# Two low-rank projections side by side, and k and r of two column blocks projected from the unnormalised input

## The chip, the cores and the metric

The kernel runs on one core of one Trainium2 chip. The metric is the device time of one execution in microseconds (us). A core has a matrix engine (TensorE, PE in the profile; its weight loads are listed apart as PEld), three engines for elementwise work (VectorE = DVE, ScalarE = ACT, GpSimd = POOL), and SyncE (SP), which here only starts transfers (DMA). Each engine runs its own instructions in the order in which they were compiled and waits on semaphores for the others.

## The reference, cut to what matters

One block of a streaming encoder on x of 512 tokens by 1024 channels, all in float32:

```python
h  = rms_norm(x, norm1_g)                # y = x * rsqrt(mean(x*x) + 1e-6) * g
p  = h @ w_in                            # all projections of three branches
# branch a: gated short convolution (3 taps);  branch b: RG-LRU (4 tap convolution, gates, scan)
# branch c: RWKV-7 with 16 heads of 64, and its columns are token-shifted first
def token_shift(p, mu):
    prev = jnp.pad(p, ((0, 0), (1, 0), (0, 0)))[:, :-1]
    return p + (prev - p) * mu
r, k, v, xw, xa, xg = _split(pc, (1024, 1024, 1024, 64, 64, 128))
w_log = -softplus(-(w0 + tanh(xw) @ w2)) - 0.5   # decay = exp(-exp(w_log))
a = sigmoid(a0 + xa @ a2)
g = sigmoid(xg) @ g2
kk = k * k_k / norm_per_head(k * k_k);  k = k * (1 + (a - 1) * k_a)
# recurrence over tokens, state of 64x64 per head; then head norm, gates, merge of the branches,
# w_out, residual, second RMSNorm, MLP with squared ReLU (1024 -> 4096 -> 1024), final RMSNorm
```

The columns xw and xa together are one block of 128 columns, the low-rank block lr0; xg is the other, lr1. RMSNorm multiplies every token by one number, so a projection may be taken on x times the gain alone and multiplied by that number afterwards.

## The kernel before, in words

**Layout.** Activations are transposed, 128 channels on the partitions and 512 tokens along the free axis. Eight such tiles (kt = 0 to 7) make up the input xT. Float32 products are made from two parts per operand, hi and lo: `mm3` (lines 169 to 171) issues hi by hi, hi weight by lo input, lo weight by hi input. One projection of 128 columns is 8 kt by 3 = 24 matmuls of 128x512. Its weight is one transfer of 128x1024 (512 KB) started by SP (`load_w`), then split: ACT casts `whi` (L148), DVE subtracts to get `wlo` (L105). There are two buffers for `raw`, three each for `whi` and `wlo`.

**Helpers.** `tt` and `stt` record every tensor-tensor and scalar-tensor-tensor operation of DVE, so all of these have line 105 or 108, and a reader goes by tile names. `proj_raw` projects the input times its gain (`xgh`, `xgl`); `unscaled` multiplies the result by `rsb`, the per-token factor of the norm, and `shift` applies the token shift (one ACT operation, one DVE operation). `proj` is the ordinary projection, of the normalised `hh` and `hl`, which `pro_scale` makes: two DVE operations and one ACT operation per kt.

**The prologue (lines 207 to 383).** Two warm-up matmuls (`wu`) run on a zero tile. Per kt, ACT makes `xgh` and the square `sq`, DVE makes `xgl`; the squares of two kt are added (DVE) and summed over channels by a float32 matmul with ones into `pst`: four such matmuls. The squares and their matmuls stand under a raised priority. The three matmuls of lr0 follow per kt. The second low-rank weight is loaded after all of xT, and its projection (lr1) runs after that of lr0. Then `rsqrt_rows` turns `pst` into `rsb`. k0 and r0 (block 0 of k and r) are projected by `proj_raw`; lr0's result is evacuated (tile us0, shifted into `lr`), and `lws` and `las`, the hi and lo inputs of the second low-rank stage, are made from it (four operations over ACT and DVE). Then `pro_scale`, the evacuation of lr1 (us1), of k0 and of r0 follow.

**krv, and what is woven into it.** `krv(g)` prepares k, r, v of the 4 heads of group g, in column blocks j = 2g and 2g+1. Per block it projects k and r (not for j = 0), computes decay and a from `lws` and `las` with four matmuls (`pw`, `pa`), the head norm of k (`pn`), and products of these; then it projects v for two blocks, sums `pb`, transposes v (`pV`), and writes its results to buffers in memory. `amat(g)` makes the per-chunk matrices of the group (tile `AXt`, evacuated in two halves of four operations each), `inverse` inverts triangles, `chain` runs the recurrence. `ab(q)` is the work of branches a and b, 8 column blocks in 232 steps; it serves as filler.

**What sets the order.** The program is written as generators; `weave(crit, fill, r)` lets r filler steps follow each step of the critical generator, which gets a raised priority. The compiler's scheduler orders each engine's instructions by priority. R0 = 0.85 is the ratio for `weave(krv(0), ab)`.

**Other pieces at the start.** POOL clears a zero tile `zer`, and four transfers (L874) fill a quarter of the buffer `ttd` with zeros from it; the scheduler has put them at the very start. Near the end of the source, `ac.activation(epst, epst, AF.Sqrt)` and a memset (L1056, L1057) stand before the last stage; the scheduler has put the activation, with its table load, at the start as well. PSUM has three buffers for projections (tag pp), two for small results (pm), and one each of pu, pS and py.

## Time and profile before

| | |
|---|---|
| time, median of 3 runs | 1028.8 us (1027.36 to 1030.81) |
| profiled execution | 1029.49 us, of which the span of the profile is 1027.7 us |
| PE | 1007.2 us busy (98%), 6110 instructions |
| PEld | 817.7 us (80%) |
| DVE | 735.1 us (72%), 1251 instructions |
| ACT | 512.9 us (50%), 757 instructions |
| POOL | 110.1 us (11%), 179 instructions |
| DMA | 151.53 MB, mean 147 GB/s |

A row such as "7.57 1.75 PE L274 MATMUL pst<-sq,ones ... x2 [2.62 <-DVE sq L105]" of the timeline gives the start, the length, the engine, the line, the operation with output and inputs, the shapes, the count of instructions put together, and in brackets the idle time just before and what ended it. Rows of the windows give start and end of a stretch, its length, and for PE, PEld, DVE, ACT and POOL the busy time with the number of instructions, then the granted TensorE clock (1.00 is full speed), the mean busy share of the 16 DMA engines and GB/s. In the list of waits a row gives engine, tile and line, what ended the wait, the idle time, how often, and the longest single one. Consecutive matmuls overlap in the records: a length of 0.39 us goes with a start every 0.23 us.

### The profile page before, as it was taken

The page shows a single profiled execution, that of the slowest core. Times are in us where ns is not written, and L with a number is a line of the kernel's source. Part 1 is how long each engine was busy: PE and PEld are TensorE (multiplying, and loading weights), DVE is VectorE, ACT ScalarE, POOL GpSimd, SP SyncE. Part 2 cuts the span into 40 slices and gives each one's busy share as a digit, 9 for nine tenths or more (in the row PEclk, how much of TensorE's full clock was granted, in tenths as well). Part 3 has the DMA queues.
Part 4 walks back from the last instruction along what each step waited for, and adds up shares of the span by engine and source line. Part 5 has one row for each costly group of instructions (what it writes and reads, how often), then busy time and mean ns, then how long its engine had stood idle before and what let it go on. Part 6 is the DMA issues. An engine that isn't in the chain of part 4 may idle for free. (4 is left out here: it accounts for less than half of the span.)

```text
span 1027.7 us, 15699 instructions
## 1 busy us (share of the span) xinstructions
PE 1007.2 (98%) x6110; PEld 817.7 (80%) x6110; DVE 735.1 (72%) x1251; ACT 512.9 (50%) x757; POOL 110.1 (11%) x179
## 2 busy tenths in 40 slices
PE   8999999999999999999999999999999999999997
PEld 5777877888887788888787877888888888878885
DVE  6997497599865886794668779656554546887775
ACT  7756453655554655456446344435433334454344
POOL 1013011201212112001322100100000000000001
PEclk9999999999999999999999999999999999999999
DMA  6444643734546446434897724544333325644442
GB/s 231 129 123 112 185 134 114 215 107 128 150 134 164 136 126 161 158 95 122 268 256 243 220 87 119 174 132 130 90 99 103 98 87 164 226 127 139 143 166 102
DMA packets 49177, 151.53 MB, mean 147 GB/s; under 512 B 6544, under 2 KB 10128, under 8 KB 48080
## 3 DMA queue, kind: packets, MB, share of 16 engines
q1 hardware_dynamic: 34816, 99.93, 30.6%
q0 software_dynamic: 13568, 49.56, 18.0%
q8 instruction: 48, 0.79, 0.3%
q10 hardware_dynamic: 720, 1.05, 0.3%
q14 instruction: 25, 0.20, 0.1%
HBM read 123.78 MB, written 26.74 MB: 146 GB/s over the span
## 5 line engine op out<-in xcount | busy, mean ns | idle before, releaser
L148 ACT CAST whi<-raw 128x1024 fp32r<-128x1024 f32 (+1 forms) x164 | 169.7, 1037 | 257.0 <-PE pp L170 86.7
L105 DVE TENSOR_TENSOR wlo<-raw,whi 128x1024 fp32r<-128x1024 f32 (+1 forms) x176 | 206.5, 1175 | 91.2 <-ACT whi L148 90.6
L169 PE MATMUL pp<-hh,whi 128*128 128x512 f32 x688 | 271.2, 395 | 0.4 <-DVE rs L108 0.4
L170 PE MATMUL pp<-hl,whi 128*128 128x512 f32 x688 | 270.1, 393 | 0.0
L171 PE MATMUL pp<-hh,wlo 128*128 128x512 f32 x688 | 269.1, 391 | 0.2 <-DVE wlo L105 0.2
L169 PEld LDWEIGHTS pp<-hh,whi 128*128 128x128 f32 x688 | 129.1, 188 | 28.9 <-DVE rs L108 0.9
L171 PEld LDWEIGHTS pp<-hh,wlo 128*128 128x128 f32 x688 | 129.2, 188 | 27.5 <-DVE wlo L105 0.6
L170 PEld LDWEIGHTS pp<-hl,whi 128*128 128x128 f32 x688 | 129.2, 188 | 26.3
L169 PE MATMUL p<-h2h,whi 128*128 128x512 f32 x256 | 100.4, 392 | 0.0
L171 PE MATMUL p<-h2h,wlo 128*128 128x512 f32 x256 | 99.7, 389 | 0.0
L170 PE MATMUL p<-h2l,whi 128*128 128x512 f32 x256 | 99.6, 389 | 0.0
L108 DVE SCALAR_TENSOR_TENSOR r<-p,rsb 128x512 f32<-128x512 f32 x32 | 22.0, 691 | 69.3 <-PE p L171 68.8
L171 PEld LDWEIGHTS p<-h2h,wlo 128*128 128x128 f32 x256 | 48.1, 188 | 10.2
L169 PEld LDWEIGHTS p<-h2h,whi 128*128 128x128 f32 x256 | 48.1, 188 | 9.8
L170 PEld LDWEIGHTS p<-h2l,whi 128*128 128x128 f32 x256 | 48.1, 188 | 9.6
L1225 POOL TENSOR_TENSOR x0f<-xr,fgt 128x512 f32<-128x512 f32 x4 | 5.2, 1296 | 310.6 <-DMA raw<-in_w 301.4
L170 PE MATMUL acc<-ml,whi 128*128 128x512 f32 x64 | 25.0, 391 | 0.0
L171 PE MATMUL acc<-mh,wlo 128*128 128x512 f32 x64 | 25.0, 390 | 0.0
L1076 PE MATMUL acc<-whi,a2h 128*128 128x512 f32 x64 | 24.9, 389 | 0.0
L1076 PE MATMUL acc<-whi,a2l 128*128 128x512 f32 x64 | 24.9, 389 | 0.0
L1076 PE MATMUL acc<-wlo,a2h 128*128 128x512 f32 x64 | 24.9, 389 | 0.0
L1076 PE MATMUL acc<-whi,ah 128*128 128x512 f32 x64 | 24.9, 389 | 0.0
(368 smaller groups left out, 1733.5 us busy)
## 6 DMA issues: line engine op xcount, KB each, us to landing
raw<-in_win SPq DMA_DIRECT2D x88, 512.0 KB, 3.6
raw<-in_w SPq DMA_DIRECT2D x64, 512.0 KB, 3.6
ax<-axd POOLq DMA_DIRECT2D x8, 1024.0 KB, 10.0
axd<-AXt POOLq DMA_DIRECT2D x12, 512.0 KB, 8.7
raw<-in_w SPq DMA_DIRECT2D x24, 256.0 KB, 2.9
bkd<-BKT POOLq DMA_DIRECT2D x4, 1024.0 KB, 15.4
raw<-in_wout SPq DMA_DIRECT2D x8, 512.0 KB, 3.6
bk<-bkd POOLq DMA_DIRECT2D x7, 512.0 KB, 13.0
```

Of the source, the lines that this page charges most:

```text
L105: return v.tensor_tensor(out=o, in0=a, in1=b, op=op)
L108: return v.scalar_tensor_tensor(out=o, in0=a, scalar=s, in1=b, op0=op0, op1=op1)
L148: ac.copy(hi[:, sl], raw[:, sl])
L169: pe.matmul(ps, wh, xh, start=start, stop=False)
L170: pe.matmul(ps, wh, xl, start=False, stop=False)
L171: pe.matmul(ps, wl, xh, start=False, stop=stop)
L1076: pe.matmul(b[i], x_[:, ms], w_, start=id(b[i]) not in begun, stop=last and n == 2, skip_group_check=True)
L1225: gp.tensor_tensor(out=o0, in0=x0, in1=fgt[0], op=MUL)
```

## The change: what it does

1. The ratio R0 goes from 0.85 to 1.8. The warm-up matmuls go from 2 of 512 columns to 12 of 128.
2. Both low-rank weights are loaded first (one half through ACT's queue) and projected side by side inside the loop over kt; the squares come after them in each kt, without a raised priority, and are added in fours: two `pst` matmuls in place of four, six additions in place of four.
3. k and r of block 1 are projected in the prologue by `proj_raw`, evacuated by `unscaled` and `shift` into two tiles, and `krv(0)` uses them in place of projections of its own. The `vs` tiles, which share those tiles' buffers, are made later.
4. The zero fill of `ttd` is taken from a new tile `zz` and stands after `krv(0)`.
5. The activation with Sqrt on `epst` and its memset are gone.

```diff
--- before.py
+++ after.py
@@ -27,8 +27,8 @@
 N_KRV = 22
 FILL = {1: (4, 13, 5), 2: (36, 13, 5), 3: (4, 13, 5)}
 
-R0, R1, R2, R3 = 0.85, 0.8, 0.85, 1.6
-NWARM = 2
+R0, R1, R2, R3 = 1.8, 0.8, 0.85, 1.6
+NWARM = 12
 
 NL = 2
 NPAIR, NPS = 12, 8
@@ -240,39 +240,56 @@
     gp.memset(ones, 1.0)
     n1t = pro.tile([P, KT], F32, name="n1t")
     ac.dma_start(n1t, par[:, PI["n1"]])
-    wlr = [new_w()]
-    load_half(wlr[0], win[CN[("lr", 0)]], 0)
-    for a, n in ((0, 1), (1, 1), (2, 2)):
+    wlr = [new_w(), new_w()]
+    lr_src = [win[CN[("lr", i)]] for i in range(2)]
+
+    def load_lr(eng, i, h):
+        sl = slice(h * S, (h + 1) * S)
+        eng.dma_start(wlr[i][0][:, sl], lr_src[i][:, sl])
+
+    def load_x(a, n):
         sy.dma_start(xT[:, a:a + n], xt[a:a + n].rearrange("k p t -> p k t"))
-    load_half(wlr[0], win[CN[("lr", 0)]], 1)
-    for a, n in ((4, 2), (6, 2)):
-        sy.dma_start(xT[:, a:a + n], xt[a:a + n].rearrange("k p t -> p k t"))
-    wlr.append(new_w())
-    for i in range(2):
-        load_half(wlr[1], win[CN[("lr", 1)]], i)
+
+    load_lr(sy, 0, 0)
+    load_lr(ac, 1, 0)
+    load_x(0, 1)
+    load_x(1, 1)
+    load_x(2, 2)
+    load_lr(sy, 0, 1)
+    load_lr(sy, 1, 1)
+    load_x(4, 2)
+    load_x(6, 2)
     gp.memset(epst[:, 0:1], EPS)
     one = cp.tile([P, 1], F32, name="one")
     gp.memset(one, 1.0)
     wu = pc.tile([P, S], F32, tag="pu", name="wu")
     for i in range(NWARM):
-        pe.matmul(wu, ones, zer, start=True, stop=True)
+        pe.matmul(wu[:, 0:P], ones, zer[:, 0:P], start=True, stop=True)
     pst = pm.tile([P, S], F32, tag="pm", name="pst")
     warm = pro.tile([P, 1], F32, name="warm")
     ac.activation(warm, epst[:, 0:1], AF.Tanh)
 
-    t_lr0 = pp.tile([P, S], F32, tag="pp", name="pp")
+    t_lr = [pp.tile([P, S], F32, tag="pp", name="pp") for _ in range(2)]
+    t_lr0, t_lr1 = t_lr
     sqp_ctx = ExitStack()
     sqp = sqp_ctx.enter_context(tc.tile_pool(name="sqp", bufs=1))
     for kt in range(KT):
-        sq = (p1 if kt % 2 else sqp).tile([P, S], F32, tag=f"v{kt // 2 % 2}" if kt % 2 else f"sq{kt // 2}", name="sq")
+        if kt % 4 == 0:
+            for w in wlr:
+                split_w(w, slice(kt // 4 * S, kt // 4 * S + S))
         ac.activation(xgh(kt), xT[:, kt], AF.Copy, scale=n1t[:, kt:kt + 1])
         stt(xgl[:, kt], xT[:, kt], n1t[:, kt:kt + 1], f(xgh(kt)), MUL, SUB)
-        with tc.high_priority(offset=OFFP):
-            ac.activation(sq, xT[:, kt], AF.Square)
-            if kt % 2 == 1:
-                tt(sq, sq, sq_, ADD)
-                pe.matmul(pst, ones, sq, start=kt == 1, stop=kt == KT - 1)
-        mm3(t_lr0, *wslice(wlr[0], kt), xgh(kt), xgl[:, kt], start=kt == 0, stop=kt == KT - 1)
+        for w, t in zip(wlr, t_lr):
+            mm3(t, *wslice(w, kt), xgh(kt), xgl[:, kt], start=kt == 0, stop=kt == KT - 1)
+        sq = (p1 if kt % 2 else sqp).tile([P, S], F32, tag=f"v{kt // 2 % 2}" if kt % 2 else f"sq{kt // 2}", name="sq")
+        ac.activation(sq, xT[:, kt], AF.Square)
+        if kt % 2 == 1:
+            tt(sq, sq, sq_, ADD)
+        if kt % 4 == 3:
+            tt(sq, sq, sq4, ADD)
+            pe.matmul(pst, ones, sq, start=kt == 3, stop=kt == KT - 1)
+        if kt % 4 == 1:
+            sq4 = sq
         sq_ = sq
     with tc.high_priority(offset=OFFP):
         rsqrt_rows(pro, rsb, pst, EPS, 1.0 / D)
@@ -341,8 +358,6 @@
         tt(o, t, rsb, MUL)
         return o
 
-    t_lr1 = pp.tile([P, S], F32, tag="pp", name="pp")
-    proj_raw(wlr[1], t_lr1)
     omul = p1.tile([P, 2], F32, name="omul")
 
 
@@ -362,6 +377,12 @@
     proj_raw(load_w(win[CN[("k", 0)]]), t_k0)
     t_r0 = pc.tile([P, S], F32, tag="pS", name="r0")
     proj_raw(load_w(win[CN[("r", 0)]]), t_r0)
+    t_kr1 = []
+    with tc.high_priority(offset=400):
+        for n in "kr":
+            t = pp.tile([P, S], F32, tag="pp", name="pp")
+            proj_raw(load_w(win[CN[(n, 1)]]), t)
+            t_kr1.append(t)
     ac.activation(lr[0:64], lr[0:64], AF.Tanh)
     lws = p1.tile([P, S], F32R, name="lws")
     las = p1.tile([P, S], F32R, name="las")
@@ -381,6 +402,9 @@
     shift(unscaled(t_k0, "us0"), pv("mu_k", 0), dvp(OMK, 0), k0)
     r0 = WP("rs")
     shift(unscaled(t_r0, "us1"), pv("mu_r", 0), dvp(OMR, 0), r0)
+    kr1 = [p1.tile([P, S], F32, tag=f"v{i}", name=f"kr{i}") for i in range(2)]
+    for i in range(2):
+        shift(unscaled(t_kr1[i], f"us{i}"), pv(("mu_k", "mu_r")[i], 1), dvp((OMK, OMR)[i], 1), kr1[i])
     pro_ctx.close()
 
 
@@ -422,11 +446,10 @@
     def krv(g, G_):
         G_.AR = pk.tile([P, 2, NC, 2, L], F32, tag="AR", name="AR")
         G_.BK = pk.tile([P, 2, NC, 2, L], F32, tag="BK", name="BK")
-        vs = [p1.tile([P, S], F32, tag=f"v{h}", name=f"v{h}") for h in range(2)]
         for jj in range(2):
             j = 2 * g + jj
-            if j == 0:
-                ks, rs = k0, r0
+            if j < 2:
+                ks, rs = (k0, r0) if j == 0 else kr1
             else:
                 ks, rs = WP("ks"), WP("rs")
                 t = yield from proj(("k", j))
@@ -435,7 +458,7 @@
             ac.activation(sq, ks, AF.Square, scale=pv("kk", j))
             sqh, sql = split(pk, sq, "b")
             yield
-            if j:
+            if j >= 2:
                 t = yield from proj(("r", j))
                 shift(t, pv("mu_r", j), dvp(OMR, j), rs)
             swh, swl = load_sw(pk, "swa", j, 0, 2)
@@ -488,6 +511,7 @@
                              G_.AR[64 * h:64 * h + 64, jj, :, 0])
             gp.dma_start(rtd[:, :, g, jj].rearrange("c p t -> p c t"), G_.AR[:, jj, :, 1])
         rk = [split(pk, rk[h], ("a1", "a3") if h else "b") for h in range(2)]
+        vs = [p1.tile([P, S], F32, tag=f"v{h}", name=f"v{h}") for h in range(2)]
         for h in range(2):
             q = 2 * g + h
             t = yield from proj(("v", q))
@@ -870,8 +894,10 @@
 
     weave(krv(0, GS[0]), fl, R0)
 
+    zz = p1.tile([P, 2, 2, P], F32, tag="vt", name="zz", bufs=2)[0:32, 0, 0, 0:32]
+    gp.memset(zz, 0.0)
     for g in range(NG):
-        gp.dma_start(ttd[32:64, g, :, 0:32], zer[0:32, 0:32].unsqueeze(1).to_broadcast([32, NC * 4, 32]))
+        gp.dma_start(ttd[32:64, g, :, 0:32], zz.unsqueeze(1).to_broadcast([32, NC * 4, 32]))
     for g in range(NG):
         if g:
             fgr = fill_group(g)
@@ -1053,8 +1079,6 @@
                 for x_ in wait_:
                     relu2_row(*x_)
                 wait_.clear()
-        ac.activation(epst, epst, AF.Sqrt)
-        gp.memset(epst, EPS)
 
         h2_ctx.close()
         with tc.tile_pool(name="fin", bufs=1, side="right") as fin:
```

On PE, at the start of the program, the order before (`wu` warm-up, `pst` sum of squares, `pp` projection of lr0):

```order
L258 MATMUL wu<-zer,ones 128x512 x2
L274 MATMUL pst<-sq,ones 128x512
L169 MATMUL pp<-xgh,whi 128x512
L170 MATMUL pp<-xgl,whi 128x512
L171 MATMUL pp<-xgh,wlo 128x512
L169 MATMUL pp<-xgh,whi 128x512
L274 MATMUL pst<-sq,ones 128x512
```

and now:

```order
L267 MATMUL wu<-zer,ones 128x128 x12
L169 MATMUL pp<-xgh,whi 128x512 x2
L170 MATMUL pp<-xgl,whi 128x512
L171 MATMUL pp<-xgh,wlo 128x512
L170 MATMUL pp<-xgl,whi 128x512
L171 MATMUL pp<-xgh,wlo 128x512
```

The first `pst` matmul no longer stands ahead of the projections; two projections go through the first kt together.

On PE, where the second low-rank stage (`pa`) of block 0 stands. Before, projections of the normalised input (`hh`) stand around it:

```order
L169 MATMUL pp<-hh,whi 128x512
L170 MATMUL pp<-hl,whi 128x512
L171 MATMUL pp<-hh,wlo 128x512
L449 MATMUL pa<-las,swah 128x512
L450 MATMUL pa<-las,swal 128x512
L169 MATMUL pp<-hh,whi 128x512 x2
```

Now (`r_326` is r0, and the `pp` behind is r of block 1):

```order
L171 MATMUL r_326<-xgh,wlo 128x512
L466 MATMUL pw<-lws,swah 128x512
L467 MATMUL pw<-lws,swal 128x512
L472 MATMUL pa<-las,swah 128x512
L473 MATMUL pa<-las,swal 128x512
L169 MATMUL pp<-xgh,whi 128x512
```

`pa` still stands behind some 120 matmuls; what surrounds it are projections of the unnormalised input.

On DVE, where the two halves of `AXt` of group 0 are evacuated (names with u and g are tiles of `ab`). Before:

```order
L105 TENSOR_TENSOR wlo<-raw,whi 128x1024
L105 TENSOR_TENSOR AXt<-pA,mask 128x2x4x64 x4
L105 TENSOR_TENSOR u_896<-u_896,g_577 128x512
L108 SCALAR_TENSOR_TENSOR g_577<-u_896,u_726 128x512
L105 TENSOR_TENSOR AXt<-pA,mask 128x2x4x64 x4
L108 SCALAR_TENSOR_TENSOR u_884<-u_902,u_884 128x512
L802 MEMSET u_884 128x1
```

and now:

```order
L826 MEMSET u_856 128x1
L105 TENSOR_TENSOR u_613<-u_613,u_856 128x512
L108 SCALAR_TENSOR_TENSOR g_931<-g_794,part,g_931 128x511
L829 SCALAR_TENSOR_TENSOR u_880<-u_865,u_613 128x512
L105 TENSOR_TENSOR wlo<-raw,whi 128x1024
L108 SCALAR_TENSOR_TENSOR g_622<-g_622,u_880 128x512
L105 TENSOR_TENSOR AXt<-pA,mask 128x2x4x64 x4
```

The memset of `ab`, which follows a square root on ACT, and the scan (L829, L805 before) stood behind both halves of `AXt` and now stand ahead of them.

## The prediction

> **What bounds the kernel now.** I read the page's head first, then windows of 10 us, the list of waits of PE, and the timeline of the start.
>
> ```profile
> span 1027.7 us, 15699 instructions
> PE 1007.2 (98%) x6110; PEld 817.7 (80%) x6110; DVE 735.1 (72%) x1251; ACT 512.9 (50%) x757; POOL 110.1 (11%) x179
> ```
>
> PE is busy for 1007.2 of 1027.7 us. The change removes no projection and no part of a later stage, so all it can gain is idle time of PE, 20.5 us over the span, and only what of this lies where the change acts. Where that is, the windows tell:
>
> ```profile
> 0.00:10.00 10.00, 5.92 (x9) 2.47 (x9) 2.40 (x4) 7.17 (x13) 4.73 (x14) 0.90 0.79 252
> 10.00:20.00 10.00, 9.87 (x35) 6.23 (x33) 9.02 (x17) 9.02 (x17) 0.14 (x2) 0.93 0.73 234
> 20.00:30.00 10.00, 10.00 (x45) 8.08 (x44) 9.96 (x32) 6.80 (x10) 0.00 (x0) 1.00 0.60 211
> 30.00:40.00 10.00, 10.00 (x44) 7.82 (x43) 9.74 (x14) 5.49 (x8) 0.58 (x1) 1.00 0.38 116
> 40.00:50.00 10.00, 10.00 (x45) 7.72 (x44) 9.93 (x21) 9.45 (x15) 0.00 (x0) 1.00 0.25 68
> 50.00:60.00 10.00, 9.59 (x43) 7.59 (x41) 9.94 (x28) 5.20 (x9) 0.91 (x1) 1.00 0.42 137
> 80.00:90.00 10.00, 9.72 (x69) 7.52 (x68) 8.29 (x13) 5.28 (x9) 3.69 (x7) 1.00 0.53 153
> 90.00:100.00 10.00, 8.88 (x66) 6.94 (x67) 7.58 (x12) 6.13 (x11) 1.88 (x3) 1.00 0.36 109
> ```
>
> 4.1 us of idle PE lie in the first 10 us. From 20 to 50 us PE has none, but DVE stands at 9.74 to 9.96 of 10: there PE and DVE run neck and neck, and whoever gains on one alone meets the other. In 50 to 60 PE is idle 0.41 us, in 80 to 90 0.28, in 90 to 100, where `amat(0)` falls, 1.12. The waits by cause:
>
> ```profile
> PE pst L274 <- DVE sq L105: 2.6, 1, 2.6
> PE pB L551 <- DVE AXt L105: 2.3, 3, 1.1
> PE wu L258 <- POOL one L255: 1.5, 1, 1.5
> PE pn L455 <- ACT a L446: 1.2, 1, 1.2
> ```
>
> The largest is that of the first sum of squares, and it stands in front of the first projection:
>
> ```profile
> 1.46 3.49 PE L258 MATMUL wu<-zer,ones 128*128 128x512 f32 x4 [1.46 <-POOL one L255]
> 7.57 1.75 PE L274 MATMUL pst<-sq,ones 128*128 128x512 f32 x2 [2.62 <-DVE sq L105]
> 13.17 1.02 PE L274 MATMUL pst<-sq,ones 128*128 128x512 f32 x2
> 6.83 0.69 DVE L105 TENSOR_TENSOR sq<-sq 128x512 f32<-128x512 f32 x1 [6.83 <-ACT sq L271]
> 4.29 0.61 ACT L271 ACTIVATE sq<-xT 128x512 f32<-128x512 f32 x1
> 6.70 0.60 ACT L148 CAST whi<-raw 128x512 fp32r<-128x512 f32 x1
> ```
>
> DVE does nothing before 6.83, and the first weight half is cast only at 6.70, although ACT's first square is done at 4.90.
>
> **Part 1, the head.** Now the weights' halves come first in the orders of ACT and DVE, and no `pst` stands ahead of the projections. The first cast can start when its half has landed. The half is issued ahead of the first tile of xT, which was there by 4.29; I take 3.9. One cast (0.6) later DVE starts, at about 4.6 in place of 6.83: 2.2 us earlier.
>
> How much of that reaches the end depends on who is next. The first matmul that needs all the early work of DVE is `pa`, which reads `las`:
>
> ```profile
> 38.78 0.69 DVE L105 TENSOR_TENSOR las<-ks,las 64x512 fp32r<-64x512 f32 x1
> 39.50 0.69 DVE L105 TENSOR_TENSOR us<-pp,rsb 128x512 f32<-128x512 f32 x1
> 39.14 0.39 PE L171 MATMUL pp<-hh,wlo 128*128 128x512 f32 x1
> 39.52 0.50 PE L449 MATMUL pa<-las,swah 128*128 128x512 f32 x1
> 39.85 0.40 PE L450 MATMUL pa<-las,swal 128*128 128x512 f32 x1
> 40.09 0.66 PE L169 MATMUL pp<-hh,whi 128*128 128x512 f32 x2
> 25.96 1.22 DVE L105 TENSOR_TENSOR wlo<-raw,whi 128x1024 fp32r<-128x1024 f32 x1
> ```
>
> `las` ended at 39.47, `pa` began at 39.52, 0.38 after the matmul before it where the usual step is 0.23: DVE set this start. Ahead of `las` the new order of DVE has two more additions of squares (0.60 each from start to start, from the step of `las` to `us` less a little) and one more full `wlo` (1.1): 2.3 us more. With the start 2.2 us earlier, `las` comes 0.1 us later, at 39.6, and `us1`, next behind it, ends at 40.3 (39.50 + 0.69 + 0.1).
>
> On PE I count the fp32r matmuls ahead of `pa`. Before: 96 of four raw projections, 15 on `hh`, 2 of `pw`, 113 in all. Now: 48 of the two low-rank projections, 24 each for k0, k1 and r0, 2 of `pw`, 122. So PE waits at `pa`. Behind `pa` comes r1, in the PSUM buffer of lr1, free when `us1` has read it: 40.3. That is the 125th matmul. Before, the 116th started at 40.09 (the pair's first), so the 125th at 40.09 + 9 x 0.23 = 42.1. **The head gains 42.1 - 40.3 = 1.8 us.** Bounds: if PE were held by nothing, it would start at 5.2 (first `wlo` done) and come to its 125th after 124 x 0.231, two `pst` of about 0.9 each (half of the pair's 1.75) and 1.1 for k1's wait for the buffer of lr0: 36.8, a gain of 5.3. If DVE starts no sooner, `las` comes at 41.8 and the 125th at 42.5: a loss of 0.4.
>
> The start has a second resource, the clock and the transfers:
>
> ```profile
> 4.00:5.00 1.00, 0.95 (x2) 0.00 (x0) 0.00 (x0) 0.89 (x3) 0.47 (x1) 1.00 0.78 154
> 5.00:6.00 1.00, 0.00 (x0) 0.00 (x0) 0.00 (x0) 0.00 (x0) 0.00 (x0) 1.00 0.85 205
> 6.00:7.00 1.00, 0.00 (x0) 0.00 (x0) 0.17 (x1) 0.83 (x2) 0.00 (x0) 1.00 1.04 387
> 8.00:9.00 1.00, 1.00 (x3) 0.34 (x1) 0.78 (x2) 0.73 (x2) 0.33 (x1) 0.50 1.07 356
> 11.00:12.00 1.00, 1.00 (x4) 0.62 (x4) 0.51 (x1) 0.99 (x2) 0.00 (x0) 0.82 1.12 381
> ```
>
> The granted clock fell to 0.50 after PE's pause and rose again in the twelfth us: a stretch of 8 to 11.4 at half speed, worth up to 1.7 us of matmuls. In the sum it costs nothing, since the DVE chain holds the end of the head either way; without that hold it takes the 5.3 down to 3.6. [...]
>
> At 4 to 6 us the transfers moved 154 and 205 GB/s, later 350 to 400. The zero fill runs in that stretch, and moves behind `krv(0)`; the second weight's halves take its place (0.5 MB more ahead of the end of xT). I let these cancel.
>
> **Part 2, k1 and r1 early, more filler.** 48 matmuls move from `krv(0)` to the prologue, at the same number; steps on `xgh` were 0.231 us against 0.2275 on `hh`: +0.2 us. DVE pays two `unscaled` (0.69 each) more. `krv(0)` has 14 steps in place of 20, and R0 = 1.8 gives 25 filler steps for 17: two filler projections more, which stand in for what left. They are missing later from the chain's cover, 35 steps left instead of 43, with the gate projections behind them; nothing runs dry there, so 0. In `krv(0)` the head norm `pn` now comes sooner after ACT's work; the one row of such a wait is the 1.2 us of `pn` above. I take 1.2, less the waits of 0.41 and 0.28 that I expect to go: **+0.5** (bounds -0.7 and +1.2).
>
> **Part 3, amat(0).**
>
> ```profile
> 90.82 2.47 DVE L105 TENSOR_TENSOR AXt<-pA,mask 128x512 f32<-128x512 f32 x4
> 95.20 2.48 DVE L105 TENSOR_TENSOR AXt<-pA,mask 128x512 f32<-128x512 f32 x4
> 101.29 0.06 DVE L802 MEMSET u<- 128x1 f32 x1 [3.02 <-ACT u L801]
> 102.11 1.22 DVE L805 TENSOR_TENSOR_SCAN u<-u,u 128x512 f32<-128x512 f32 x1
> ```
>
> The memset that waited 3.02 us for ACT's square root stood behind both halves of `AXt`; now it, the scan and a `wlo` stand ahead of them. Two more filler projections, 11 us of PE work, stand ahead as well, so most of that wait should be over when the first half is due. I take **+0.4** (bounds 0 and +3.3, below).
>
> **Part 4, what is hidden.** Two `pst` fewer (0.9 us each) lie in the stretch that DVE holds: 0. The fill of `ttd` now costs POOL
>
> ```profile
> 8.67 0.79 POOL L874 DMA_DIRECT2D ttd<-zer  x1 [4.20 <-issue]
> ```
>
> 0.79 us each, 3.2 for four, behind the transfers of `krv(0)` and ahead of those of `amat(0)`; POOL is busy 1.88 of 10 us there and only `inverse`, a stage later, reads them: 0, or 3.2 if that cover is gone. The Sqrt at the start takes a table load with it, and the load that it made necessary later:
>
> ```profile
> 2.88 1.28 ACT L1056 ACT_TABLE_LOAD   x1
> 23.35 1.28 ACT L391 ACT_TABLE_LOAD   x1
> 24.64 0.21 ACT L391 ACTIVATE spt<-spt 128x8 f32<-128x8 f32 x1
> ```
>
> The first ended at 4.16, before the first square could start (4.29), the second lies where ACT is busy for 6.80 of 10: both 0. [...]
>
> All else, the waits of some 5 us between 100 and 650 us, is only put in another order (0, give or take 1.5); from the output projection on the instructions are the same.
>
> **Sum:** -1.8 + 0.2 + 0.5 + 0.4 = -0.7. The profiled execution took 1029.49 us, 1.8 over its span; by the sum it would take 1028.8. It lies 0.7 over the median of the runs, 1028.8, so the time of runs comes to 1028.1.
>
> **The rivals.** *PE sets the pace of the head.* If DVE's chain to `las` is shorter than I added up (it had some 1 us idle in 10 to 20), PE keeps all it saved: -5.3 + 1.1 = -4.2, 1024.6; with the slow clock as before, 1026.3. For it speaks that DVE was not yet full there; against it the full rows from 20 to 50.
>
> *AXt falls behind the square root.* Mechanism: DVE stands at the memset for up to 3.0 us, then does scan, `wlo` and three small operations (1.2 + 1.2 + 1.2) before `AXt`: 6.6 us late. PE covers 1.4 with the six filler matmuls between the halves, and 1.9 was spare between the halves (95.20 - 90.82 - 2.47): +3.3, in place of the +0.4: 1031.0. It decides from the point where ACT's square root ends later than the first `pA` by over 3 us. Against it: the extra filler.
>
> *The change does not do what it says.* The first halves land late because two of them share the transfers, and the head begins where it did: +0.4 + 1.1, 1030.3.
>
> **How the numbers follow.** Forecast as summed 0.47 (its own range 1026 to 1030), PE-paced head 0.30, AXt late 0.13, head unchanged 0.10. A measurement of this kernel tells 0.3%, 3.1 us, from no change: 1025.7 to 1031.9. Faster: 0.26 of the 0.30 and 0.09 of the forecast's, 0.35. Slower: 0.05 of the 0.13, with later waits 0.9 or more to the bad, and 0.05 spread over the forecast's and the last, 0.10. Same: 0.55. The range reaches from 1023.0 (PE-paced, with later waits 1.5 better) to 1031.4.
>
> **What would show it.** In the profile after: DVE's first work before 5 us and no wait at `pst` in front of the projections (part 1); PE idle of 2 to 3 us in front of `pa`, which ends with `las` at 39 to 40 us (the hold; PE without idle there means the PE-paced rival); an idle of about 1 us at `pn` and not over 2 us in `amat(0)`. If `pB` waits 4 us or more, the AXt rival is right; if the first projection starts after 7 us, the last one is.

## The result: 0.85% slower, and the profile after

The changed kernel took 1037.5 us (median of 6 runs), the kernel before beside it 1029.6: a ratio of 1.0085, 95% interval 1.0059 to 1.0111. In a second comparison of the same two kernels it was 1.0057 (1.0038 to 1.0076). The forecast was 1028.1 with a range of 1023.0 to 1031.4. So the change makes the kernel some 6 to 8 us slower, and not one of the cases of the prediction gave that much.

The first profile after is of the slowest of the six executions (1043.0 us, span 1041.2). Its head:

```profile
span 1041.2 us, 15741 instructions
PE 1015.3 (98%) x6126; PEld 826.8 (79%) x6126; DVE 739.3 (71%) x1255; ACT 510.1 (49%) x754; POOL 109.7 (11%) x179
```

Two things grew: PE's idle time, from 20.5 to 25.9 us, and PE's busy time, from 1007.2 to 1015.3 us, although the new order holds hardly more work. The same matmuls took longer. The waits of PE after the change (engine, tile and line, what ended the wait; total, times, longest):

```profile
PE pu L679 <- DMA ax<-axd: 2.5, 1, 2.5
PE pa L472 <- DVE las L105: 2.4, 1, 2.4
PE pB L575 <- DVE AXt L105: 1.8, 3, 0.9
PE pA L553 <- DVE AXt L105: 1.7, 2, 1.2
PE pn L478 <- ACT a L469: 1.5, 1, 1.5
...
PE pp L169 <- DVE us L105: 1.0, 1, 1.0
```

The 2.6 us at `pst` are gone. New are 2.4 us at `pa`, 1.0 at k1's buffer, 1.7 at `pA`, and 2.5 in the chain.

**Where the time went.** A comparison by the clock on the wall misleads here, since eight more filler steps stand early. I count PE's work instead: the start of the n-th matmul of 128x512, warm-ups and `pst` left out, after minus before, in us (worked out from all PE rows of the two traces; in kernels with ten added matmuls these are left out too). The second profile is of a run of 1034.8 us. In between, where transposes and other small matmuls stand in another place, the difference swings; the rows shown are those where it is steady (from 900 on, the small matmuls done up to each row are the same in number, too).

| n-th matmul | at (before), us | first profile | second profile |
|---|---|---|---|
| 40 | 22.3 | -5.1 | -5.3 |
| 120 | 41.0 | -3.1 | -2.9 |
| 140 | 45.6 | +2.7 | +1.4 |
| 280 | 78.9 | +1.8 | +0.6 |
| 900 | 240.2 | +0.4 | +0.7 |
| 1300 | 345.3 | +1.4 | +1.8 |
| 1700 | 444.6 | +5.2 | +5.1 |
| 2400 | 661.8 | +12.6 | +5.6 |
| 3900 | 1007.8 | +13.5 | +5.3 |

The head leads by 2.9 to 3.1 us up to `pa`, and loses 4 to 6 us in the next twenty matmuls. By matmul 900 it is nearly even. Then 4.3 to 4.9 us are lost between 900 and 1700, the stages of groups 2 and 3, in both profiles alike. In the first profile alone 7 us more go in the chain.

**What happens at pa.** PE around it, and windows of 4 us (PE, PEld, DVE, ACT, POOL busy; then the granted clock):

```profile
38.56 0.40 PE L467 MATMUL pw<-lws,swal 128*128 128x512 f32 x1
41.40 0.79 PE L472 MATMUL pa<-las,swah 128*128 128x512 f32 x1 [2.44 <-DVE las L105]
42.41 0.63 PE L169 MATMUL pp<-xgh,whi 128*128 128x512 f32 x1
```

```profile
36.00:40.00 4.00, 2.96 (x13) 1.84 (x11) 3.94 (x7) 2.38 (x3) 0.00 (x0) 1.00 0.42 133
40.00:44.00 4.00, 2.60 (x6) 2.08 (x7) 3.70 (x7) 1.75 (x4) 0.00 (x0) 0.59 0.40 131
44.00:48.00 4.00, 4.00 (x11) 3.06 (x11) 4.00 (x7) 3.45 (x6) 0.00 (x0) 0.56 0.12 33
48.00:52.00 4.00, 4.00 (x19) 3.24 (x18) 2.02 (x4) 2.11 (x4) 0.70 (x1) 1.00 0.00 0
```

PE waits 2.44 us for `las`. Then the granted clock is at 0.50 from about 40.7 to 47.6: PE is busy for all of 44 to 48 and gets through 11 matmuls where it gets through 19 at full clock. The pause is paid twice, once as idle time and once as slow matmuls, which the profile counts as busy. The same pair of events stands in the chain of the first profile, and not in that of the second, whose chain lost 0.5 us there:

```profile
524.00:528.00 4.00, 1.48 (x30) 1.00 (x28) 0.79 (x2) 1.10 (x2) 2.36 (x5) 1.00 1.02 259
528.00:532.00 4.00, 3.25 (x49) 2.39 (x46) 0.68 (x1) 0.58 (x1) 0.43 (x1) 0.60 1.04 287
532.00:536.00 4.00, 4.00 (x58) 3.69 (x56) 0.68 (x1) 0.27 (x1) 0.00 (x0) 0.50 1.03 266
536.00:540.00 4.00, 4.00 (x13) 3.15 (x12) 0.00 (x0) 0.69 (x2) 0.00 (x0) 0.62 0.52 164
```

**Why las is late.** DVE after:

```profile
4.33 0.69 DVE L105 TENSOR_TENSOR wlo<-raw,whi 128x512 fp32r<-128x512 f32 x1 [4.33 <-ACT whi L148]
6.24 0.69 DVE L105 TENSOR_TENSOR wlo<-raw,whi 128x512 fp32r<-128x512 f32 x1 [1.22 <-ACT whi L148]
...
20.87 0.71 DVE L195 STREAM_TRANSPOSE rqw<-pst 128x512 f32<-128x512 f32 x1
...
23.97 0.71 DVE L202 STREAM_TRANSPOSE rsb<-rqq 128x512 f32<-128x512 f32 x1
25.47 1.22 DVE L105 TENSOR_TENSOR wlo<-raw,whi 128x1024 fp32r<-128x1024 f32 x1 [0.79 <-ACT whi L148]
26.61 0.68 DVE L105 TENSOR_TENSOR us<-pp,rsb 128x512 f32<-128x512 f32 x1
...
39.41 1.22 DVE L105 TENSOR_TENSOR wlo<-raw,whi 128x1024 fp32r<-128x1024 f32 x1
40.65 0.69 DVE L105 TENSOR_TENSOR las<-ks,las 64x512 fp32r<-64x512 f32 x1
```

and before:

```profile
15.80 0.72 DVE L195 STREAM_TRANSPOSE rqw<-pst 128x512 f32<-128x512 f32 x1
...
23.02 0.71 DVE L202 STREAM_TRANSPOSE rsb<-rqq 128x512 f32<-128x512 f32 x1
...
24.76 0.68 DVE L105 TENSOR_TENSOR us<-pp,rsb 128x512 f32<-128x512 f32 x1
```

DVE starts 2.5 us earlier, as forecast. But its second operation waits for the second weight's half, and it first reads `pst` 5 us later than before, so `rsb` is 0.95 us late, the next `wlo` waits 0.79 us for ACT, and `us0` is 1.85 us late. `las` ends at 41.34 against 39.47: from `us0` to there DVE takes 14.7 us in both kernels, so all of the delay is made ahead of `us0`.

### The profile page after: what moved, and what is told of

It is laid out like the page before. It is cut to its first block, busy times and chain, and to the rows that moved or that the text cites. A ratio compares the mean times of both kernels' runs of the same rounds, so it can differ in the third digit from the quotient of the medians.

```text
span 1041.2 us, 15741 instructions
## 1 busy us (share of the span) xinstructions
PE 1015.3 (98%) x6126; PEld 826.8 (79%) x6126; DVE 739.3 (71%) x1255; ACT 510.1 (49%) x754; POOL 109.7 (11%) x179
## 4 chain that ended last, share of the span: by engine, by line
PE 55%; DVE 5%; DMA 4%; ACT 3%; issue 1%; POOL 0%; DVEq 0%; ACTq 0%
PE acc L1100 14%; PE pp L169 6%; PE pp L170 6%; PE pp L171 6%; PE p L169 5%; PE p L171 5%; PE p L170 5%; DMA rt<-rtd 2%; DMA raw<-in_win 1%; PE py L689 1%; DVE wlo L105 1%; PE acc L169 1%; PE acc L171 1%; PE acc L170 1%; DVE ym L105 1%
## 5 line engine op out<-in xcount | busy, mean ns | idle before, releaser
L169 PE MATMUL pp<-hh,whi 128*128 128x512 f32 x672 | 266.2, 396 | 0.0
L171 PE MATMUL pp<-hh,wlo 128*128 128x512 f32 x672 | 264.1, 393 | 0.4 <-DVE wlo L105 0.4
L170 PE MATMUL pp<-hl,whi 128*128 128x512 f32 x672 | 264.4, 393 | 0.0
L169 PEld LDWEIGHTS pp<-hh,whi 128*128 128x128 f32 x672 | 126.7, 189 | 27.8 <-ACT u L796 0.2
L171 PEld LDWEIGHTS pp<-hh,wlo 128*128 128x128 f32 x672 | 126.7, 189 | 27.5 <-DVE wlo L105 1.0
L170 PEld LDWEIGHTS pp<-hl,whi 128*128 128x128 f32 x672 | 126.9, 189 | 25.9
L171 PEld LDWEIGHTS p<-h2h,wlo 128*128 128x128 f32 x256 | 48.0, 188 | 10.2
L169 PE MATMUL acc<-mh,whi 128*128 128x512 f32 x64 | 24.8, 395 | 1.1 <-ACT gc L768 0.7
```

The costliest lines, as they stand in the source:

```text
L169: pe.matmul(ps, wh, xh, start=start, stop=False)
L170: pe.matmul(ps, wh, xl, start=False, stop=False)
L171: pe.matmul(ps, wl, xh, start=False, stop=stop)
```

## The experiments

Each is timed beside the kernel before on its own chip; ratios are to that.

### The changed kernel again

> The changed kernel once more, unaltered, for a second profile. Theory 1 (clock): the wait of 2.4 us at pa, behind las, is in every execution and takes the granted clock to 0.50 for some 6 us behind it, about 2.9 us of matmul time; the second drop of the profiled execution (after the wait of 2.5 us of pu for the ax transfer in the chain, 10 us at 0.50, about 5 us) belongs to that execution alone, which took 1043.0 where the others took 1035.7 to 1038.1. Expected: about 1037.5, one drop at 41 us, none in the chain. Rival (order): the chain's wait comes with the new order of the work and is in this profile too, over 2 us, with its drop.

1035.8 us, 1.0057 (1.0038 to 1.0076). One clock drop at 41 us as theory 1 said, here half as long as in the first profile (3.4 us against 6.8), and none in the chain, so that one belonged to the first execution. The window behind `pa`, with the clock ahead of the last two numbers:

```profile
40.00:44.00 4.00, 2.38 (x6) 1.86 (x7) 3.91 (x6) 1.55 (x4) 0.00 (x0) 0.63 0.42 131
```

Theory 1 did not foresee two things in this profile: a short drop at 187 us (3.4 us), behind a wait of 1.3 us at `pA`, and the 4 us lost between matmul 900 and 1700. That loss is in both profiles, and no drop stands beside it.

### The wait at pa filled

```diff
             pe.matmul(pw, swl[:, 0], lws, start=False, stop=True)
+            if j == 0:
+                keep = pc.tile([P, S], F32, tag="pu", name="keep")
+                for _ in range(10):
+                    pe.matmul(keep, lws[:, 0:P], lws, start=True, stop=True)
```

> The changed kernel with ten matmuls on lws, whose result nobody reads, between pw and pa of block 0: they fill the wait at pa, so PE does not pause; las and everything behind it stand where they stood. Theory 1 (clock): pa starts at 41.4 as before, the clock stays at 1.00 behind it, and the time falls by 2.9 us, to about 1034.6. Rival: the clock drop costs nothing because DVE sets the pace there, and the time stays at 1037.5.

1032.2 us, 1.0009 (0.9989 to 1.0030): 3.6 us under the changed kernel on the same chip. Of this kernel:

```profile
38.78 2.47 PE L471 MATMUL keep<-lws 128*128 128x512 f32 x10
41.39 0.50 PE L476 MATMUL pa<-las,swah 128*128 128x512 f32 x1
...
40.00:44.00 4.00, 3.86 (x16) 2.56 (x15) 3.94 (x7) 1.93 (x4) 0.00 (x0) 1.00 0.42 131
```

`pa` starts where it did (41.39 against 41.40), nothing useful was done earlier, and the clock stays at 1.00. The drop behind the wait is a cost of its own: at matmul 280 this kernel is 0.6 us ahead of the kernel before where the two profiles of the changed kernel are 0.6 and 1.8 us behind, so the drop costs 1.2 us where it lasts 3.4, and 2.4 where it lasts 6.8. The wait itself only takes back what the head had gained (3.1 us ahead at matmul 120, 0.2 behind at 140). From there to matmul 900 it gains a further 1.6 us on the second profile of the changed kernel, which has a like source: the drop at 187 us of that profile is not in this one. The remaining 0.8 of the 3.6 us no profile shows; it is within the noise. At matmul 900 the kernel is 2.1 us ahead; between 900 and 1700 it loses 4.5 us like the changed kernel.

### The filler ratio back at 0.85

```diff
-R0, R1, R2, R3 = 1.8, 0.8, 0.85, 1.6
+R0, R1, R2, R3 = 0.85, 0.8, 0.85, 1.6
```

> The changed kernel with the filler ratio of krv(0) back at 0.85. If the loss between matmul 1200 and 2400 (amat of the last groups and the chain, some 8 to 11 us in the first profile) comes from filler that was used up early, it goes: 1030 to 1033, although krv(0) itself may wait more. If it comes from the head alone, the time stays at 1036 to 1039.

1038.9 us, 1.0081 (1.0056 to 1.0107). Neither expectation fits: with 14 steps the ratio 0.85 does not give back the 17 filler steps of before, `krv(0)` runs bare (3.1 us at a projection of the filler, 2.5 at `pn`, a clock drop of 3.4 us with each), and the later stages meet a third place in the filler, where they lose 0.4 us between matmul 900 and 1700. It shows that 14 steps need more than 0.85. It also shows a wait of 2.45 us at `pa` without a drop behind it:

```profile
38.00:42.00 4.00, 1.55 (x6) 0.81 (x6) 3.94 (x7) 1.86 (x4) 0.00 (x0) 1.00 0.32 77
42.00:46.00 4.00, 4.00 (x19) 3.26 (x18) 4.00 (x8) 3.53 (x7) 0.00 (x0) 1.00 0.30 109
```

### The squares' priority back

The squares, their sums and the two `pst` matmuls of the changed kernel stand again inside `with tc.high_priority(offset=OFFP):`.

> The changed kernel with the raised priority back around the squares, their sums and the two pst matmuls. In the changed profile rsb is ready at 24.7 us against 23.7 before, and las at 41.3 against 39.5, although DVE starts 2.5 us earlier. If the dropped priority made rsb late, las comes 1 to 1.5 us earlier, the wait at pa is about 1 us, the clock stays up, and the time falls by 3 to 4 us, to about 1034. If DVE's total of work ahead of las sets it, las stays within 0.5 us of 41.3 and the time at 1037.

1035.2 us, 1.0041 (1.0024 to 1.0058). `las` ends at 39.21, 2.1 us earlier, the wait at `pa` is 0.31 us and the clock stays up, as expected (mean 0.997 over the run, against 0.990 and 0.996 in the two profiles of the changed kernel). The reason was another: `rsb` comes at 24.85, no sooner than in the changed kernel (24.68). `us0` comes 0.7 us sooner, and one full `wlo` now stands behind `las` and not ahead of it:

```profile
24.14 0.71 DVE L202 STREAM_TRANSPOSE rsb<-rqq 128x512 f32<-128x512 f32 x1
24.77 1.18 DVE L105 TENSOR_TENSOR wlo<-raw,whi 128x1024 fp32r<-128x1024 f32 x1
25.88 0.68 DVE L105 TENSOR_TENSOR us<-pp,rsb 128x512 f32<-128x512 f32 x1
...
38.52 0.69 DVE L105 TENSOR_TENSOR las<-ks,las 64x512 fp32r<-64x512 f32 x1
...
39.85 1.22 DVE L105 TENSOR_TENSOR wlo<-raw,whi 128x1024 fp32r<-128x1024 f32 x1
```

At matmul 900 the kernel leads by 2.5 us; between there and 1700 it loses 5.0, and 2.3 more behind it. In time it gained only 0.6 us on the changed kernel where the filled wait gained 3.6, and why its end is the worse of the two stays open. So a second cause was left, and theory 1 alone had fallen. The new theory: the **phase of the filler**. `ab` has 29 steps per column block; the changed kernel takes 25 in `krv(0)` where the kernel before took 17, so groups 2 and 3 meet other pieces of it.

### The filler's phase restored, and imposed

Three kernels with R0 = 1.22 (17 steps in `krv(0)` as before), so that from `amat(0)` on PE, DVE and ACT have the order of the kernel before; and the kernel before with the phase of the changed one.

```diff
-R0, R1, R2, R3 = 1.8, 0.8, 0.85, 1.6
+R0, R1, R2, R3 = 1.22, 0.8, 0.85, 1.6
```

> The changed kernel with the filler ratio 1.22: krv(0) has 14 steps now where it had 20, so 1.22 gives 17 filler steps in it, as many as before the change, and from amat(0) on the instructions of PE, DVE and ACT stand in the order of the kernel before. Theory (two causes): the head with its clock drop costs 1 to 2 us at equal work, the other 4 us or so come from the filler's phase against the later stages; expected 1.0 to 2.0 us over the kernel before, and from matmul 900 to 2400 no further loss. Rival (head alone): the later loss follows from the delay itself, and the time stays at 1035.8.

> The changed kernel with the raised priority back around squares, sums and pst, and the filler ratio 1.22. By the two causes both losses are gone: at equal work it was 2.3 us ahead of the kernel before at matmul 900 with the raised priority, and nothing is lost later: 1027.5 to 1029, against 1030.2 of the kernel before. By the rival (the later loss does not hang on the phase) it stays at 1034 to 1035.

> The changed kernel with the ten unread matmuls ahead of pa and the filler ratio 1.22. By the two causes 1.5 to 2.3 us under the kernel before, like the run with the raised priority: the clock stays up, las as late as in the changed kernel. If the clock drop had come back elsewhere, or the later loss stayed, 1032.

> The kernel before with nothing changed but the filler ratio of krv(0), 1.25 for 0.85: with its 20 steps this gives 25 filler steps, as the changed kernel has, and from amat(0) on the instructions of PE, DVE and ACT stand in the order of the changed kernel. By the filler's phase it loses 3 to 5 us against the kernel before between matmul 900 and 2400, with the waits at pA, pB and pn that the changed kernel shows there; time 1033 to 1035. By the rival it stays at 1030.

| kernel | us | ratio (95%) |
|---|---|---|
| changed, 1.22 | 1034.7 | 1.0032 (1.0013 to 1.0050) |
| changed, squares' priority, 1.22 | 1031.1 | 1.0001 (0.9983 to 1.0019) |
| changed, wait filled, 1.22 | 1030.6 | 1.0001 (0.9982 to 1.0020) |
| before, 1.25 | 1037.2 | 1.0059 (1.0040 to 1.0078) |

The last row is the plainest. One number, changed in the kernel before and with none of the rest, makes it about as slow as the whole change does. (It came out slower than expected; its profile also has a drop of 3.4 us at 105.6, behind a wait of 0.94 at `pA` in `amat(0)`.) All four agree on the stretch between matmul 900 and 1700: the first three lose nothing there (changes of 0.1 us or less), the last 4.3 us. With the phase restored, both remedies for the wait at `pa` show in the time: 3.6 and 4.2 us under the first row, which has neither. The window from 300 to 420 us (PE, PEld, DVE, ACT, POOL) of, in this order, the kernel before, the changed kernel, the changed with 1.22, and the kernel before with 1.25:

```profile
300.00:420.00 120.00, 118.40 (x626) 96.59 (x625) 81.03 (x131) 65.21 (x94) 19.24 (x28) 1.00 0.55 153
```
```profile
300.00:420.00 120.00, 115.32 (x608) 93.21 (x607) 81.71 (x132) 63.00 (x92) 20.87 (x31) 1.00 0.50 134
```
```profile
300.00:420.00 120.00, 118.42 (x629) 96.72 (x629) 79.76 (x129) 63.32 (x93) 20.89 (x31) 1.00 0.56 155
```
```profile
300.00:420.00 120.00, 115.88 (x610) 93.66 (x609) 82.27 (x133) 63.55 (x94) 20.85 (x31) 1.00 0.50 134
```

PE's busy time and count fall into two pairs, and what the kernels of a pair share is the phase.

What these runs did not bear out: the first was expected 1 to 2 us over the kernel before and is 4 over; its profile has a second drop, at 96.7 behind a wait of 2.6 at `pA`. And the two whose wait at `pa` was short or filled were expected under the kernel before, and came out equal to it. They lead by 2.2 and 1.3 us at matmul 240 and have lost it by 320, in the end of `krv(0)`. One row of the kernel with the priority, two of that with the filled wait:

```profile
77.53 0.50 PE L169 MATMUL pp<-hh,whi 128*128 128x512 f32 x1 [1.50 <-ACT u L797]
```
```profile
78.04 0.50 PE L527 MATMUL pb<-bh,bd 128*128 128x512 f32 x1 [1.26 <-ACT bh L164]
79.57 0.51 PE L169 MATMUL pp<-hh,whi 128*128 128x512 f32 x1 [1.03 <-ACT u L800]
```

Behind the last two the clock fell to 0.50 from 80.8 to 84.2. `u` is a tile of the filler: with fewer filler steps, as I read it, PE comes sooner to a projection whose buffer ACT has not yet emptied.

### Where the phase bites, and phase against amount

The kernel before with `FILL` for group 2 at (44, 13, 5) for (36, 13, 5), which leaves everything up to group 2 as it was; and the kernel before with R0 = 2.3, one whole column block of filler more.

> The kernel before with eight more filler steps ahead of group 2 (lead 44 for 36) and nothing else: up to there its order is that of the kernel before, behind it that of the changed kernel. At equal work the changed kernel and the kernel before with the ratio 1.25 lose 4 to 5 us between matmul 1100 and 1600. If that loss is the phase of the filler at groups 2 and 3, this kernel loses the same there, and some more in the chain: 1034.5 to 1036.5. If it is the phase at groups 0 and 1, or comes with the head, the time stays at 1030.7.

> The kernel before with the filler ratio 2.3, 46 filler steps in krv(0): 29 more than before, one whole column block of the branches a and b (232 steps over 8 blocks), so later stages meet the same pieces of a block as before, one block later. By the phase alone the loss between matmul 1100 and 1600 is within 1 us of none, and the time 1030 to 1032, if krv(0) bears the denser filler. If it is the amount of filler used early (29 steps fewer for the chain), it loses more than with the ratio 1.25: 1040 or more, from matmul 1900 on.

The first took 1035.7 us, 1.0057 (1.0043 to 1.0070). At equal work it stands where the kernel before does up to matmul 1100 (0.7 us, which it had from its start), and loses 4.9 us from there to 1700. The phase at groups 2 and 3 is the place. `amat(3)` of this kernel on DVE and PE:

```profile
402.70 0.69 DVE L108 SCALAR_TENSOR_TENSOR g<-u,u 128x512 f32<-128x512 f32 x1
403.31 2.48 DVE L105 TENSOR_TENSOR AXt<-pA,mask 128x512 f32<-128x512 f32 x4
405.71 0.68 DVE L108 SCALAR_TENSOR_TENSOR u<-u,u 128x512 f32<-128x512 f32 x1
406.31 1.53 DVE L108 SCALAR_TENSOR_TENSOR g<-g,part,g 128x511 f32<-128x511 f32 x2
407.75 2.48 DVE L105 TENSOR_TENSOR AXt<-pA,mask 128x512 f32<-128x512 f32 x4
...
404.05 3.02 PE L529 MATMUL pA<-AR,BK 64*128 64x128 f32 x32
409.09 1.97 PE L551 MATMUL pB<-ident,BK 128*128 128x128 f32 x16 [0.88 <-DVE AXt L105]
```

and of the kernel before on DVE:

```profile
387.65 2.48 DVE L105 TENSOR_TENSOR AXt<-pA,mask 128x512 f32<-128x512 f32 x4 [1.75 <-PE pA L529]
391.23 2.48 DVE L105 TENSOR_TENSOR AXt<-pA,mask 128x512 f32<-128x512 f32 x4 [1.09 <-PE pA L529]
```

Before, DVE was idle ahead of each half of `AXt` and waited for PE. With the other phase the filler's gate arithmetic (`u`, `g`) stands ahead of and between the halves, and PE waits for DVE. In the same way a cast of the filler holds ACT ahead of `pn` (1.39 us there). Of the 4.9 us, 3.0 are idle time of PE; 1.8 are in rows of `pA`, which count as busy and are longer (3.02 us above, against 2.06 in the kernel before): the weight loads of `pA` wait for `AXt` in steps there, 2.6 us in six waits against 0.7 in two.

The second took 1045.0 us, 1.0155 (1.0134 to 1.0176): at matmul 900 and at 1700 it is 1.0 us ahead of the kernel before, so a whole block more does not cost what 8 steps cost, and the phase stands. But the filler is then missing at the end of the chain, as the amount's theory said:

```profile
648.37 0.69 PE L725 MATMUL pYt<-ident,Y 128*128 128x128 f32 x2 [9.37 <-DVE Y L105]
```

### The head without k1 and r1, and the phase mended later

> The changed kernel with k and r of block 1 back in krv(0), as projections of the normalised input, and the ratio back at 0.85: left are the two low-rank projections side by side, the small warm-ups, the moved zero fill and the removed Sqrt. The order from amat(0) on is that of the kernel before. pa stands behind fewer raw projections. Theory: las comes late as in the changed kernel (41 us), PE waits for it, and the clock falls: 0 to 3 us over the kernel before. Rival (k1 and r1 early make the wait, since they put 24 more matmuls on the input side of it): no wait at pa over 1 us, and 1 to 2 us under the kernel before.

1035.9 us, 1.0060 (1.0041 to 1.0079). Neither reading held. With k1 and r1 back there is no wait at `pa`, so their early projections do make it; but the kernel is no faster. It leads by 4.4 us at matmul 80, loses that ahead of `pa` in waits for `hl` and `lws`, and then:

```profile
63.09 0.50 PE L169 MATMUL pp<-hh,whi 128*128 128x512 f32 x1 [3.17 <-ACT g L783]
```

A projection in `krv(0)` waits 3.2 us for ACT to empty a buffer of the filler, a clock drop stands behind it (the mean clock of the run is 0.996), and the loss is 4.6 us by matmul 280, and 3.6 from 320 to 1700.

> The changed kernel with the raised priority back around the squares, R0 = 1.8 kept (25 filler steps in krv(0)), and eight filler steps fewer ahead of group 2 (lead 28 for 36), so that from group 2 on the order is that of the kernel before. With the raised priority alone it stood 2.3 us ahead at equal work up to matmul 900 and lost it between 1100 and 1600. By the phase this loss is gone and the lead stays: 1028 to 1029, some 0.2% under the kernel before. If the later stages lose it anyway, 1031 or more.

1038.0 us, 1.0081 (1.0067 to 1.0096). From matmul 1100 to 2400 it loses nothing, as the phase says. It lost 8 us just before, in `inverse(0)`, which the lead steps of group 2 are woven into: eight fewer leave a matmul of it bare.

```profile
271.65 0.58 PE L622 MATMUL pG<-dg,Z 32*32 32x32 f32 x13 [3.12 <-ACT a L476]
```

A wait of 3.1 us, and the clock at 0.50 for 10 us behind it.

### Both causes mended

The eight steps taken off around group 1 (`FILL` 1: (1, 13, 0) for (4, 13, 5)), with R0 = 1.8, once with the squares' priority and once with the ten matmuls; and the kernel without k1 and r1 with the squares' priority.

> The changed kernel with the raised priority back around the squares, R0 = 1.8, and eight filler steps fewer around group 1 (lead 1 for 4, gap 0 for 5), so that from the end of group 1 on the order is that of the kernel before; the 36 steps that cover the inverse stay. By the phase the lead of 2.3 us at matmul 600 to 900 is kept: 0.1 to 0.25% under the kernel before. If fewer steps around group 1 open waits there, or the clock drops, no gain: equal to the kernel before or over it.

> The changed kernel with the ten unread matmuls ahead of pa, R0 = 1.8, and the same eight filler steps fewer around group 1. By the phase and the clock together its time is 1.5 to 2.5 us under the kernel before; by a later loss that has another cause it stays at 1.0009 of it, as with the ten matmuls alone.

> The changed kernel with k and r of block 1 back in krv(0), the ratio back at 0.85, and the raised priority back around the squares. The same kernel without that priority lost 4 us before matmul 240 (a wait of 3.2 us for ACT's g of the filler, and the clock drop behind it) and none later. If rsb and las coming late push ACT's and DVE's filler work, the wait goes with the priority: 0 to 2 us under the kernel before. If the side-by-side projections themselves move the filler against krv(0), it stays some 0.4% over.

With the priority: 1031.4 us, 1.0004 (0.9986 to 1.0022), as the second reading above has it; the lead of 2.5 us at matmul 240 is gone by 700, in waits of 0.86 at the end of `krv(0)`, 0.89 in `amat(0)`, and 0.54, 0.97 and 1.17 us in group 1.

With the ten matmuls: **1027.3 us, 0.9965 (0.9949 to 0.9981)**, under both kernels, and 3.1 us under the kernel before where 1.5 to 2.5 was expected. Its lead at 900 is only 0.4 us (it has the same three waits of group 1); the other 3.8 us of this profile, taken in the fastest of its twelve runs, appear in the chain and behind it, where it shows no wait of PE behind 380 us and the kernel before shows 3.2 us of them. From 177 us on its PE, DVE and ACT work in the order of the kernel before, so no order explains this, and I have no cause to name. Against the kernel before, the kernels with that same order moved by -3.8 to +2.7 us behind matmul 1700 in their single profiles, and this result, the best of fourteen altered kernels, was not repeated. No clock drop stands between the warm-up and the end, and the mean clock of all twelve is 0.997 or 0.998.

The kernel without k1 and r1: 1037.0 us, 1.0049 (1.0026 to 1.0072); the wait of 3.17 us for `g` is there again, so the squares' priority is not its cause. Which piece of the side-by-side projections sets it up stays open.

## Why the prediction was wrong, by its own steps

**The head's start** was right: DVE began at 4.33 (forecast 4.6), no `pst` stands ahead of the projections. The warm-ups ran to 6.84 us and the first projection began at 6.89, and no clock drop stands there.

**"The head gains 42.1 - 40.3 = 1.8 us"**, the largest term of the sum, is the first step that failed: the 125th matmul began at 42.41 and 42.63 in the two profiles, against 42.17 before, so the head lost 0.2 to 0.5 us. `las` was forecast at 39.6 and came at 41.34. DVE started 2.5 us earlier (forecast 2.2), but its work ahead of `las` grew by 3.2 us (forecast 2.3), and its idle time there by 1.1 (2.0 to 3.1), where I added up its operations as if it never waited. The waits are those of 1.22 us for the second weight's half and 0.79 for ACT behind `rsb`; part of the uncounted work is six small operations on `spt`, which now stand ahead of `us0`. The prediction's own lower bound, "`las` comes at 41.8 and the 125th at 42.5", is near what happened, but by luck: its condition, a DVE that starts no sooner, did not hold. The wait of PE at `pa`, forecast at 2 to 3 us, was 2.44.

**"In the sum it costs nothing, since the DVE chain holds the end of the head either way"** is the second. I weighed the clock only for the start, where the old drop might go, and never asked what the new wait at `pa` would do, though I forecast its length and had the row beside it: 2.62 us of idle at `pst`, and the clock at 0.50 right behind. Filling the wait gave 3.6 us back, 1.2 to 2.4 of it by this drop. DVE's hold does not shelter the matmuls behind `pa`: PE is busy all through 44 to 48 us and does not wait for DVE there. The prediction's frame, "all it can gain is idle time of PE", took the busy time as fixed; in the first profile it grew by 8.1 us.

**"All else ... is only put in another order (0, give or take 1.5)"** is the third, and the largest: the ratio R0 alone, in the kernel before, costs 0.59% (0.40 to 0.78). I had counted whether the filler would run out (it did not) and its length, and not which pieces of it the later stages would meet.

Phase and head are not quite a sum: 0.59% and 0.32% by themselves (the latter the changed kernel with the phase restored), 0.57 to 0.85% together; the intervals allow both.

**Part 2's +0.5 and part 3's +0.4** were not borne out: at equal work `krv(0)` and `amat(0)` gave back 1 to 2 us in the changed kernel (from +2.7 at matmul 140 to +1.1 at 400 in the first profile, +1.4 to -0.2 in the second). The rival in which `AXt` falls behind the square root did not occur at group 0 (`pB` waited 0.3 us there), but its mechanism, filler arithmetic on DVE ahead of `AXt`, is what the phase does at groups 2 and 3. Of part 4, the moved zero fill, the removed Sqrt and the two `pst` fewer were not tried alone. A row of `pst` with x2 is one matmul in two records (eight records for the four of the source), so "half of the pair's 1.75" halves a single one; at full clock such a row is 1.02 us, so the 0.9 was nearly right by luck.

## What to carry to other kernels

In these runs a pause of PE in mid kernel could have two prices, its length and the slow matmuls behind it (2.44 us at `pa`, then 6.8 us at a clock of 0.50 in the first profile), and the second was booked as busy time (4.00 of 4 us for 11 matmuls where 19 go at full clock): read the granted clock behind each wait of about 1 us and more (the shortest named above with a drop behind it is 0.94 us), and fill a wait that can't be removed, as the ten matmuls did for 3.6 us. Where a ratio spreads filler over a critical chain, a change of it shifts every later stage against the filler; count the steps taken, keep them equal when something else is tried, and change them as an edit of their own. And to find where two orders of one program part, compare them at equal work, not at equal times.

## What the runs showed of the hardware

The slow stretches had only a few lengths. They were 3.4 us behind the wait of 2.62 us at the start of the kernel before, 6.8 and 3.4 behind that of 2.44 at `pa`, and 10.2 behind 2.52 in the chain and behind 3.12 at the inverse. With R0 = 2.3 a stretch of 17.1 us began behind a wait of 1.47 in the chain and had the one of 9.37 inside it. All of these are multiples of the shortest, 3.41 us (7.94 to 11.35 us in the kernel before). Nor did the wait's length alone decide: 2.45 us at `pa` in the run with the ratio 0.85 left the clock at 1.00 (the two windows shown there), and behind 1.3 us at `pA` in the second profile it fell to 0.50.

The traces also show where the drops began and ended: within one execution every change of the clock falls on one grid of 3.41 us, in the first profile at 40.73, 47.55, 528.83 and 539.07 us, in the second at 41.02, 44.44, 187.80 and 191.21. Cut along this grid, the seventeen traces (up to the last 20 us or so of each) have by my count thirteen pieces at full clock in which PE was idle for 2.0 us or more (2.62 in the kernel before, 2.33 in the chain of the first profile), and a drop begins at the end of every one; no drop stands behind a piece with less than 1.1 us. In between, a drop follows in 6 of some fifty, so idle time alone does not decide there. Both exceptions lie in that range: an edge cuts the 2.45 us of the ratio 0.85 into 1.73 and 0.72 us, and the piece with the 1.3 us at `pA` has 1.50 us of idle time in all. The changed kernel's wait at `pa` lies there too (1.77 us of it in one piece in the first profile, 1.85 in the second), and so does a piece of the first profile at 351.34 us with 1.33 us of idle time and no drop behind it.
